# Layer 1's gate projection: eight strips of 512-column matmuls in pairs by Strassen's seven block products

## The chip, the cores and the metric

The kernel runs on one core of one Trainium2 chip. The metric is the device time of one execution in microseconds (us); lower is better. Before the change three runs took 1444.09, 1445.64 and 1447.06 us, median 1445.64.

Engines are named as in the profile: PE (TensorE, matrix multiply), PEld (its loading of the stationary operand), DVE (VectorE), ACT (ScalarE), POOL (GpSimd), and SP (SyncE), whose queue issues all the DMAs that matter here.

## The reference

A trunk of two layers over a sequence of 1024 tokens, width 1024, one batch. Each layer is a pre-norm with adaLN modulation from a conditioning vector c, a mixer with a SiLU gate, an output projection and a gated residual. Layer 0 is differential attention, layer 1 multi-head latent attention:

```python
def _modulation(c, ada_w, ada_b):
    mod = jax.nn.silu(c) @ ada_w + ada_b
    shift, scale, gate = jnp.split(mod[:, None, :], 3, axis=-1)
    return shift, scale, gate
...
def _mla(h, positions, w_in, q_a_norm_g, w_q_b, kv_a_norm_g, w_kv_b, w_out):
    proj = h @ w_in
    q_a, c_kv, k_pe, z = jnp.split(proj, [384, 640, 704], axis=-1)
    q = _rmsnorm(q_a, q_a_norm_g) @ w_q_b          # 8 heads of 128 + 64
    kv = _rmsnorm(c_kv, kv_a_norm_g) @ w_kv_b      # 8 heads of 128 (k) + 128 (v)
    ...                                            # rope on q_pe and k_pe, softmax attention
    o = o.reshape(b, s, MLA_WIDTH) * jax.nn.silu(z)
    return o @ w_out
...
    x = x + gate * y
```

The matmul that the change touches is z = h @ w_z: 1024 tokens by 1024 columns, contracted over 1024.

## The kernel before

**Precision.** Every projection is computed from split operands: a float is written as hi + lo, both in the fp32r format, and `mm3` issues three matmuls, hi·hi, hi·lo and lo·hi, into one PSUM bank (L178 to L180). So each operand needs a split: ACT casts it to hi, then POOL (for weights, L223 and L224) or DVE subtracts hi from it to get lo.

**Layout.** The normed input of layer 1 lies in SBUF transposed, as `h1[k][half]`: k = 0 to 7 are blocks of 128 channels, half = 0 or 1 the first or last 512 tokens, each a pair (hi, lo) of tiles of 128 x 512. A strip of weights makes 128 output columns: two raw tiles of 128 x 512 (`wraw`, two buffers, in `wst`) are loaded, split, and multiplied with the eight k of each half: 24 matmuls of 128 x 512 to one result in PSUM. Results lie with output columns on partitions and tokens along the free axis.

**Stages of layer 1**, in the order of PE's program, on which the stages lie one behind the other:

1. *The latent strips* (`lora`, L1215 on): strip 0 is k_pe (rope follows, `kp_half`), 1 to 3 are q_a, 4 and 5 are c_kv. ACT copies each result to `craw` and squares it (`csq`), DVE adds the squares up (`csum`). After the last strip of a latent and half, `norm` sums over partitions on PE (`cps`, eight small matmuls), takes the inverse root (DVE `c_w`, POOL `rq_y`), and spreads it over all partitions by a trip through DRAM: a store `bc_d` and a broadcast load `bc_s`. Then `rest` multiplies (`craw`, DVE), and splits into hi (ACT) and lo (POOL), which stay in SBUF as `CQ` and `CK` until attention 1. The four cps stand, on PE, among the strips that follow: `half_and_norm` runs what waits in `norms` at k = 4 of the next half strip. Two fall among the c_kv strips, the third and fourth at the start of the gate strips.
2. *The gate strips* (`z1_strip`, h = 0 to 7): per half 24 matmuls, a tanh on ACT, one DVE operation that reads the result from PSUM, and a store to `zS` in DRAM. Between the strips, `gen_gate` computes layer 1's residual gate: eight loads of 512 KB and eight DVE dot products of 128 x 1024 (L428).
3. *The first half of v* (`v1_tile`, eight tiles of six matmuls): each is split into `v_hl` (three buffers) by ACT and DVE and stored to `vS` in DRAM, 512 KB a store.
4. *The first strips of attention 1*: rope part of q (`w_qr`), k and q of head 0 (`w_kn`, `w_qn`), the rest of v, and then the scores, a stream of softmax tiles in which PE transposes and multiplies without a break.

**What sets the order.** PE's work is written out in the program's text. The other engines' instructions are put into one in-order queue per engine when the program is built, by a scheduler that follows the text and the readiness of data as it models it; an engine doesn't go past an instruction that waits. SP's queue is in order as well: a DMA that waits for its source or for a free buffer holds the ones behind it.

Here is one PSUM detail that matters: strips take their banks in turn from five (two `acc`, three `accx`), so the sixth result after a given one needs its bank.

Of the kernel before, what the change touches and what calls it, by code (L numbers as in the profile page):

```python
# [27 lines left out]
NH = 8  # L28
# [50 lines left out]
def f32v(ap):  # L79
    return ap.bitcast(F32)  # L80
# [3 lines left out]
def trunk(ctx: ExitStack, tc: tile.TileContext, A, out):  # L84
# [61 lines left out]
    def part(name):  # L146
        lo, n = VEC[name]
        return vec[:, lo : lo + n]
# [1014 lines left out]
    def strip1(i, wpool=None):  # L1163
        return load_strip([A["w_s1"][i, f] for f in range(2)], [4, 4], wpool)
# [23 lines left out]


    stC = ExitStack()  # L1190
    cqp = pool(stC, "cq", side="right")
    CQ = [[(cqp.tile([P, HF], F32R, name=f"cqh{k}_{f}"), cqp.tile([P, HF], F32R, name=f"cql{k}_{f}")) for f in range(2)] for k in range(3)]
    CK = [[(cqp.tile([P, HF], F32R, name=f"ckh{k}_{f}"), cqp.tile([P, HF], F32R, name=f"ckl{k}_{f}")) for f in range(2)] for k in range(2)]
# [4 lines left out]
    st4 = ExitStack()  # L1198

    def kp_half(half, acc):  # L1200
        rot, fin = rope(wp, acc, half, 1.0)

        def g():
            rot()
            r = fin()
            hi = lr.tile([P, HF], F32R, name="kp_h", tag="kp_h", bufs=1)
            V.tensor_copy(hi, r)
            V.tensor_copy(KP[half][0:64], r[0:64])
            V.tensor_sub(KP[half][64:128], r[64:128], f32v(hi[64:128]))

        return g

    norms = []

    def half_and_norm(w, half, consume):  # L1215

        for k, _ in enumerate(gen_half(w, h1, half, consume)):
            if k == NORM_AT:
                for f in norms[:]:
                    norms.remove(f)  # L1220
                    f()

    def lora(idx, dst, gvec, width, ws=None, first=None):
        n = len(idx)
        craw = [[None, None] for _ in range(n)]
        sums = [None, None]
        def put(i, half, acc):
            t = lr.tile([P, HF], F32, name="craw", tag="craw", bufs=6)
            S.copy(t, acc)
            craw[i][half] = t  # L1230
            if i == 0:
                sums[half] = lr.tile([P, HF], F32, name="csum", tag="csum", bufs=2)
                S.activation(sums[half], acc, AF.Square)
            else:
                s2 = lr.tile([P, HF], F32, name="csq", tag="csq", bufs=1)
                S.activation(s2, acc, AF.Square)
                V.tensor_add(sums[half], sums[half], s2)

        def norm(half):
            pt = bank("tr", "cps", [P, 4, P])  # L1240
            for j in range(4):
                PE.matmul(pt[:, 0, j : j + 1], sums[half][:, j * P : (j + 1) * P], ones[:, 0:1], start=True, stop=True)
            wv = sm.tile([P, 4], F32, name="c_w")
            V.tensor_scalar(wv, pt[:, 0, 0:4], 1.0 / width, EPS, op0=ALU.mult, op1=ALU.add)
            y = rsqrt(wv, 4)
            _, rb = bcast_rows(lr, y, "cbc", 1)

            def rest():
                for i in range(n):
                    t = craw[i][half]  # L1250
                    tc.keep_in_program_order(V.scalar_tensor_tensor(
                        out=t3(t), in0=t3(t), scalar=gvec[:, i : i + 1], in1=rb, op0=ALU.mult, op1=ALU.mult))
                    hi, lo = dst[i][half]
                    S.copy(hi, t)
                    G.tensor_sub(lo, t, f32v(hi))
# [12 lines left out]

    def first_halves(put):

        g0 = kp_half(0, strip_half(w4[0], h1, 0))
        for _ in gen_half(w4[1], h1, 0, put):
            side.tick()
        side.flush()
        st3x.close()
        g0()
        kp_half(1, strip_half(w4[0], h1, 1))()

    lora((1, 2, 3), CQ, qag, QL, w4[1], first_halves)
    lora((4, 5), CK, kvg, KVL)  # L1280

    def z1_strip(h, extra=None):
        w = strip1(6 + h)
        if extra:
            extra()
        for half in range(2):
            def put(acc, half=half):
                gz = silu_gate(wp, acc)
                SP.dma_start(zS[h, half], gz)
            half_and_norm(w, half, put)  # L1290

    z1_strip(0)
    stL.close()
    stv = ExitStack()
    pv1 = pool(stv, "pv1", side="right")
    p4 = pool(st4, "p4")

    c2, c_fin = load_c(p4, p4.tile([P, D], F32, name="cth", tag="ada", bufs=2))
    c_fin()
    gates = gen_gate(1, lambda src: mod_load(src, p4, 2), c2)  # L1300
    next(gates)
    wk = [[None, None] for _ in range(2)]

    def load_wk(fh, wpool):
        for k in range(2):
            raw = p4.tile([P, HF], F32, name="wvr", tag="wvr", bufs=2)
            SP.dma_start(raw, A["w_v1"][k, fh])
            h_ = wpool.tile([P, HF], F32R, name="wvh", tag="wv1", bufs=4)
            l_ = wpool.tile([P, HF], F32R, name="wvl", tag="wv1", bufs=4)
# [9 lines left out]
            mm3(acc, ch[:, c_], cl[:, c_], wk[k][fh][0], wk[k][fh][1], k == 0, k == 1)  # L1319
        store_v(1, sp, acc, tt, fh, *buf)  # L1320

    for h in range(1, NH):
        next(gates)
# [4 lines left out]
    sth.close()  # L1328

# [74 lines left out]
    def attn1(h, fills, extra=None, late=None):  # L1404

        def open_(half):
            ctx_["gz"] = wst.tile([P, HF], F32, name="gz1", tag="gz", bufs=3)
            SP.dma_start(ctx_["gz"], zS[h, half])

        def close(half, o_, zz):  # L1410
            if late and half == 1:
                ctx_["late"] = late(o_, zz, ctx_["gz"])
                return
            o = ap.tile([P, HF], F32, name="o1", tag="o", bufs=2)
            V.scalar_tensor_tensor(out=o, in0=o_, scalar=0.5, in1=ctx_["gz"], op0=ALU.mult, op1=ALU.mult)
            V.reciprocal(zz, zz)
            finish(o, zz, 1, h, half, None, ap, None)
# [40 lines left out]
    for tt in v1_left:  # L1458
        v1_tile(tt, 1, ap, "pt", 6)
    stv.close()  # L1460
    for h in range(NH - 1):
        attn1(h, lambda i: FILL1[i])
        while late_q:
            late_q.pop(0)()
        stream1.step(sum(steps1[: h + 2]) - stream1.count)
    stw.close()
    stC.close()
    stO = ExitStack()
# [158 lines left out]
```

## Time and profile before

| what | us |
|---|---|
| median of three runs | 1445.64 |
| the profiled execution | 1448.22 |
| its span | 1446.4 |
| PE busy | 1396.9 |
| DVE, ACT, POOL busy | 858.4, 710.5, 605.0 |
| latent strips to gate strips (first cps at, first gate matmul at) | 829.7, 858.03 |
| gate strips to v (first matmul of v at) | 949.23 |
| first matmul of the qr strip | 960.43 |
| first scores of attention 1 | 985.86 |

PE's granted clock over the run was 0.995 of full speed. Times in the text are microseconds from the start of the span. In a row of a timeline the columns are start, duration, engine, line, operation, output<-inputs, partitions x elements, and in square brackets how long the engine had been idle and what released it. The line numbers before the prediction are those of the kernel before; L1216 and above in the order of the changed kernel are its own.

### The profile page before, as it was taken

Reading aid. Unit: us, or ns where it says so; the run is one execution under the profiler, and the core shown is the slowest. Engines: PE = TensorE matmul, PEld = TensorE weight load, DVE = VectorE, ACT = ScalarE, POOL = GpSimd, SP = SyncE. Lnnn points to the kernel's source line nnn. Section 1 sums busy time; section 2 is a strip of 40 time slices with the busy share of each in tenths; the row PEclk is TensorE's granted clock in tenths of the full one; section 3 lists DMA queues with packets and bytes.
Section 4 is the critical chain, followed back from the end, with each engine's and each line's share of the span. In section 5 each row is a group of like instructions: output and inputs, shape, how many; then the busy total and the mean of one; then the engine's idle time right before and its main releaser. Section 6 shows DMA issues by size and latency. Waiting matters only on the chain.

```text
span 1446.4 us, 20456 instructions
## 1 busy us (share of the span) xinstructions
PE 1396.9 (97%) x7424; PEld 1167.0 (81%) x7424; DVE 858.4 (59%) x1272; ACT 710.5 (49%) x1258; POOL 605.0 (42%) x484
## 2 busy tenths in 40 slices
PE   5999999999999999998999999998999999999997
PEld 4778788888888887887787878787888888888886
DVE  6656777767777767677344445134555555555365
ACT  5522366656565665566343332234454554545342
POOL 4416164656564655453551264321141321412473
PEclk9999999999999999999999999999999999999999
DMA  9787823333333324137653127367242332345574
GB/s 327 234 248 234 256 66 97 87 103 81 101 97 88 98 81 110 63 95 262 229 171 124 38 69 239 110 189 204 77 104 77 110 99 76 105 136 175 172 238 149
DMA packets 128470, 203.19 MB, mean 140 GB/s; under 512 B 18289, under 2 KB 55281, under 8 KB 128369
## 3 DMA queue, kind: packets, MB, share of 16 engines
q1 hardware_dynamic: 128368, 201.89, 45.6%
q8 instruction: 58, 0.95, 0.3%
q14 instruction: 44, 0.35, 0.1%
HBM read 132.68 MB, written 45.56 MB: 123 GB/s over the span
## 4 chain that ended last, share of the span: by engine, by line
PE 77%; DMA 7%; DVE 6%; ACT 3%; POOL 3%; issue 2%; SPq 2%; ACTq 0%; DVEq 0%; POOLq 0%
PE s L1397 10%; PE acc L180 8%; PE acc L179 8%; PE acc L178 8%; PE tr L376 7%; PE s L767 7%; PE pv L179 4%; PE pv L178 4%; PE pv L180 4%; PE oacc L178 4%; PE oacc L179 4%; PE oacc L180 4%; DMA ada<-in_ada_g 2%; DMA wvr<-in_w_v 2%; DMA vS<-v_hl 1%
## 5 line engine op out<-in xcount | busy, mean ns | idle before, releaser
L378 ACT CAST pth<-tr 128x512 fp32r<-128x512 f32 x256 | 150.3, 587 | 283.6 <-PE tr L376 280.0
L393 DVE TENSOR_REDUCE nm<-s 128x1 f32<-128x1024 f32 x192 | 234.0, 1219 | 73.6 <-PE s L767 64.0
L379 DVE TENSOR_TENSOR ptl<-tr,pth 128x512 fp32r<-128x512 f32 x256 | 176.2, 688 | 150.2 <-ACT pth L378 149.9
L224 POOL TENSOR_TENSOR wl<-wraw,wh 128x512 fp32r<-128x512 f32 (+2 forms) x94 | 116.8, 1244 | 243.4 <-ACT wh L223 216.2
L395 ACT ACTIVATE e<-s,nm 128x1024 f32<-128x1024 f32 x128 | 143.7, 1122 | 28.1 <-DVE nm L393 27.6
L376 PE MATMUL tr<-ident,e 128*128 128x128 f32 x1024 | 154.6, 273 | 1.9 <-DVE ptl L379 1.7
L376 PEld LDWEIGHTS tr<-ident,e 128*128 128x128 f32 x1024 | 121.5, 140 | 42.8 <-DVE ptl L379 19.2
L178 PE MATMUL acc<-h0h,wh 128*128 128x512 f32 x360 | 150.0, 417 | 2.0 <-DVE v_hl L356 1.9
L178 PE MATMUL pv<-pth,vt 128*128 128x256 f32 x512 | 147.4, 288 | 0.0
L179 PE MATMUL pv<-ptl,vt 128*128 128x256 f32 x512 | 145.5, 284 | 0.0
L180 PE MATMUL pv<-pth,vt 128*128 128x256 f32 x512 | 144.6, 282 | 0.0
L180 PE MATMUL acc<-h0h,wl 128*128 128x512 f32 x360 | 142.2, 395 | 0.5 <-POOL wl L224 0.5
L179 PE MATMUL acc<-h0l,wh 128*128 128x512 f32 x360 | 141.4, 393 | 0.0
L1007 POOL TENSOR_TENSOR wol<-wor,woh 128x512 fp32r<-128x512 f32 x64 | 85.8, 1361 | 84.4 <-ACT woh L1006 79.4
L178 PEld LDWEIGHTS pv<-pth,vt 128*128 128x128 f32 x512 | 97.6, 191 | 3.0 <-ACT pth L378 0.4
L179 PEld LDWEIGHTS pv<-ptl,vt 128*128 128x128 f32 x512 | 97.7, 191 | 2.6
L180 PEld LDWEIGHTS pv<-pth,vt 128*128 128x128 f32 x512 | 97.7, 191 | 0.1
L325 POOL TENSOR_TENSOR rp_sw<-rp_sw,sinT 128x512 f32<-128x512 f32 x42 | 55.2, 1314 | 80.6 <-DMA rp_sw<-rp_raw 77.6
L767 PE MATMUL s<-ks,qa 128*128 128x512 f32 x256 | 82.2, 402 | 3.5 <-DVE e L775 3.1
L775 DVE SCALAR_TENSOR_TENSOR e<-s,z,e 128x1024 f32<-128x1024 f32 x64 | 82.1, 1283 | 2.1
L223 ACT CAST wh<-wraw 128x512 fp32r<-128x512 f32 (+2 forms) x94 | 55.2, 587 | 55.8 <-PE acc L179 38.5
L320 POOL TENSOR_TENSOR rp_r<-rp_raw,cosT 128x512 f32<-128x512 f32 x38 | 49.4, 1302 | 78.5 <-ACT rp_raw L315 50.8
(469 smaller groups left out, 3281.7 us busy)
## 6 DMA issues: line engine op xcount, KB each, us to landing
wraw<-in_w_s SPq DMA_DIRECT2D x76, 256.0 KB, 2.8
ada<-in_ada_ss SPq DMA_DIRECT2D x32, 512.0 KB, 6.1
vS<-v_hl SPq DMA_DIRECT2D x32, 512.0 KB, 4.9
vt<-vS SPq DMA_DIRECT2D x32, 512.0 KB, 4.0
wor<-in_w_out SPq DMA_DIRECT2D x64, 256.0 KB, 3.9
rp_sw<-rp_raw SPq DMA_DIRECT2D x168, 64.0 KB, 2.0
bc_s<-bc_d SPq DMA_DIRECT2D x34, 256.0 KB, 4.0
ada<-in_ada_g SPq DMA_DIRECT2D x16, 512.0 KB, 5.2
```

The source lines that it names most:

```text
L178: PE.matmul(psum, ah, bh, start=first, stop=False)
L179: PE.matmul(psum, ah, bl, start=False, stop=False)
L180: PE.matmul(psum, al, bh, start=False, stop=last)
L224: sub = (V if pair_of else G).tensor_sub(l_[:, :n], raw[:, :n], f32v(h_[:, :n]))
L376: PE.transpose(tr[:, j, :], p[:, kt * P : (kt + 1) * P], ident)
L378: mk["S"] = S.copy(pth[kh][:, :, dst], tr).ins
L379: mk["V"] = V.tensor_sub(ptl[kh][:, :, dst], tr, f32v(pth[kh][:, :, dst])).ins
L393: mk["V"] = V.reduce_max(nm, s_ps, axis=AX.X, negate=True).ins
L395: mk["S"] = S.activation(e, s_ps, AF.Exp, bias=nm, scale=1.0, accum_out=zs).ins
L767: PE.matmul(s_ps[:, kc * HF : (kc + 1) * HF], src[:, c, ql], KS[h][kc][:, c, :], start=fst, stop=not fst)
L1007: in_turn(G.tensor_sub(lo, raw, f32v(hi)))
L1397: PE.matmul(s_ps[:, kc * HF : (kc + 1) * HF], lhs, rhs(kc), start=i == 0, stop=i == 4)
```

## The change

**The products.** The gate strips go in pairs. The contraction is cut into two halves of four k (q = 0, 1), the tokens into the two halves, and the columns of a pair into its two strips. With A = h1 (four blocks: A00 = `h1q(0,0)`, A01, A10 = `h1q(1,0)`, A11) and W (a11, a12 for the first strip, a21, a22 for the second), the four results of a pair come from seven products of four k each, in Winograd's form, in place of eight: 84 matmuls a pair, not 96. Per pair DVE makes four sums of weights from raw tiles (`z_weights`), and all seven weight blocks are split by ACT and POOL. DVE makes seven sums of results from PSUM; the first product is copied to SBUF (`zu`) by ACT; the tanh and the gating operation read sums in SBUF.

**The input sums.** Products 3 to 6 need T2, T3, T1 and T4, sums of the blocks of A, 16 tiles (hi, lo). Each `combo` takes two DVE subtractions (of the hi and of the lo parts), a DVE addition, a cast on ACT and a subtraction on POOL. They are set amid the latent strips, one a k step (`side.tick`).

**Room.** The sums take the place of `CQ` and `CK`: the latents are now split as soon as they are normed, stored to DRAM (`cS`, 20 tiles of 256 KB), and loaded again in pair 3, once products have freed tiles. The small tiles of these steps share a ring of six ("rp"). The weights of v (`load_wk`) come by way of `wraw`.

**The gate's dot products** move from between the gate strips to attention 1's heads 0 to 3: sixteen of 128 x 512, each with a load of 256 KB, two per two softmax steps, issued behind DVE's running work (`gate_steps`).

```diff
-    CQ = [[(cqp.tile([P, HF], F32R, name=f"cqh{k}_{f}"), cqp.tile([P, HF], F32R, name=f"cql{k}_{f}")) for f in range(2)] for k in range(3)]
+    TC = {n: [(ut(f"t{n}h", n == 1 and k > 1), ut(f"t{n}l", n == 1 and k > 1)) for k in range(4)] for n in (2, 3, 1)}
+    cS = dr.tile([5, 2, 2, P, HF], F32, name="cS")
...
+    def combo(dst, x, y):
+        hi, lo = dst
+        t, u = rpt("cmb_t"), rpt("cmb_u")
+        V.tensor_sub(t, f32v(x[0]), f32v(y[0]))
+        V.tensor_sub(u, f32v(x[1]), f32v(y[1]))
+        V.tensor_add(t, t, u)
+        S.copy(hi, t)
+        G.tensor_sub(lo, t, f32v(hi))
+
+    def combos():
+        for k in range(4):
+            a_, b_ = h1[k][0], h1[k + 4][0]
+            c_, d_ = h1[k][1], h1[k + 4][1]
+            combo(TC[1][k], c_, a_)
+            combo(TC[2][k], d_, TC[1][k])
+            combo(TC[3][k], d_, c_)
...
+            combo(TC[4][k], h1[k + 4][0], TC[2][k])
...
-                    hi, lo = dst[i][half]
+                    hi = rpt("c_h", F32R)
                     S.copy(hi, t)
-                    G.tensor_sub(lo, t, f32v(hi))
+                    G.tensor_sub(t.bitcast(F32R), t, f32v(hi))
+                    SP.dma_start(cS[dst + i, half, 0], f32v(hi))
+                    SP.dma_start(cS[dst + i, half, 1], t)
...
+    def z_weights():
+        for _ in range(NH // 2):
+            a11, a12 = zraw[:2]
+            yield split_raw(a11, 4)
+            yield split_raw(a12, 4)
+            a21, a22 = zraw[2:4]
...
+            V.tensor_add(s1, a21, a22)
+            V.tensor_sub(a21, a11, a21)
+            V.tensor_sub(a11, s1, a11)
+            V.tensor_sub(a12, a12, a11)
+            for t in (a11, a21, s1, a22, a12):
+                yield split_raw(t, 4)
...
+    def z_pair(p, late=lambda i: None):
+        u = rpt("zu")
+        S.copy(u, product(h1q(0, 0)))
+        acc = product(h1q(1, 0))
+        c_ = rpt("z11")
+        V.tensor_add(c_, acc, u)
+        gate_out(2 * p, 0, c_, c_)
+        V.tensor_add(u, product(TC[2]), u)
+        late(0)
...
+        acc = product(TC[3])
+        u3 = rpt("zu3")
+        V.tensor_add(u3, acc, u)
+        late(1)
+        acc = product(TC[1])
...
+        V.tensor_add(u3, product(TC[4]), u3)
+        gate_out(2 * p + 1, 0, u3, u3)
+        V.tensor_add(u, product(h1q(1, 1)), u)
+        gate_out(2 * p, 1, u, u)
...
-    for h in range(1, NH):
-        next(gates)
-        z1_strip(h, lambda: [load_wk(fh, wpool) for fh, wpool in enumerate((p4, pv1))] if h == NH - 1 else None)
+    def late_z(i):
+        if i == 0:
+            load_ck(CK, 3, [(k, half) for half in range(2) for k in range(2)])
+        if i == 1:
+            load_ck(CQ, 0, [(0, 0), (1, 0), (2, 0), (0, 1)])
+        if i == 2:
+            load_wk(0)
+            load_ck(CQ, 0, [(1, 1), (2, 1)])
+    z_pair(1)
+    load_wk(1)
+    z_pair(2)
+    z_pair(3, late_z)
```

Three places show how the change moves instructions.

DVE's queue from the end of the k_pe rope on, before (`kps` is the rope's last result, `csum` the sum of squares of which the third and fourth let the first two cps go, `c_w` what DVE does behind a cps):

```order
L1208 CAST kps_7011<-rp_r 64x512
L1209 TENSOR_TENSOR kps_7011<-rp_r,kp_h 64x512
L1237 TENSOR_TENSOR csum<-csum,csq 128x512 x2
L1244 TENSOR_SCALAR c_w<-cps 128x4
L1237 TENSOR_TENSOR csum<-csum,csq 128x512
```

and in the changed kernel (L1228 to L1230 are a combo's three operations, L1352 and L1353 sums of weights, L1280 is csum):

```order
L1216 TENSOR_TENSOR kps_7011<-rp_r,kp_h 64x512
L1228 TENSOR_TENSOR cmb_t<-h1h,h_0h 128x512
L1229 TENSOR_TENSOR cmb_u<-h1l,h_0l 128x512
L1352 TENSOR_TENSOR zs_8573<-zraw 128x512
L1230 TENSOR_TENSOR cmb_t<-cmb_t,cmb_u 128x512
L1353 TENSOR_TENSOR zraw<-zraw 128x512
L1228 TENSOR_TENSOR cmb_t<-h1h,t1h 128x512
L1229 TENSOR_TENSOR cmb_u<-h1l,t1l 128x512
L1228 TENSOR_TENSOR cmb_t<-h1h 128x512
L1230 TENSOR_TENSOR cmb_t<-cmb_t,cmb_u 128x512
L1229 TENSOR_TENSOR cmb_u<-h1l 128x512
L1280 TENSOR_TENSOR csum<-csum,csq 128x512
```

Behind these stand, up to the third csum, twelve more operations of combos and one csum; the csum of the first norm now has 24 two-input operations between itself and the last kps.

ACT's queue at pair 0 in the changed kernel (`c_h` is the hi part of a normed latent, `zu` the copy of product 1, `t4h` the hi part of T4, `wh` that of a weight block); before, there was no zu, and c_h had no result behind it that PE's banks wait for:

```order
L1231 CAST t4h<-cmb_t 128x512
L223 CAST wh<-zraw 128x512
L1279 ACTIVATE csq<-acc 128x512
L223 CAST wh<-zraw 128x512
L1297 CAST c_h<-craw 128x512 x2
L1385 COPY zu<-zacc 128x512
L1362 ACTIVATE zth<-z_8638 128x512
```

The copy of product 1 stands behind two casts that need the third norm's broadcast.

SP's queue around v, before:

```order
L202 DMA wraw<-in_w_qr 128x384
L1289 DMA zS<-gz 128x512 x2
L202 DMA wraw<-in_w_kn 128x256
L202 DMA wraw<-in_w_qn 128x384
L1289 DMA zS<-gz 128x512 x2
L202 DMA wraw<-in_w_kn 128x256
L202 DMA wraw<-in_w_qn 128x384
L1408 DMA gz_9534<-zS 128x512
L1289 DMA zS<-gz 128x512
L358 DMA vS_0_71<-v_hl 256x4x128 x8
```

and in the changed kernel (`cS` is the parked latents, `c2h` the conditioning vector for the moved dots):

```order
L1440 DMA ckh<-cS 128x512
L1440 DMA ckl<-cS 128x512
L1364 DMA zS<-zu_9203 128x512
L1364 DMA zS<-zu 128x512
L358 DMA vS_0_71<-v_hl 256x4x128 x8
L202 DMA wraw<-in_w_qr 128x384
L202 DMA wraw<-in_w_kn 128x256
L1470 DMA c2h<-in_c 128x512 x2
```

The loads of the weights of attention 1's first strips (qr, kn, qn) stood ahead of the eight stores of v; now they stand behind all eight.

More of the change, by code (lines that the diff above doesn't have):

```diff
@@ L1190, in trunk, with ut @@
     stC = ExitStack()
-    cqp = pool(stC, "cq", side="right")
-    CQ = [[(cqp.tile([P, HF], F32R, name=f"cqh{k}_{f}"), cqp.tile([P, HF], F32R, name=f"cql{k}_{f}")) for f in range(2)] for k in range(3)]
-    CK = [[(cqp.tile([P, HF], F32R, name=f"ckh{k}_{f}"), cqp.tile([P, HF], F32R, name=f"ckl{k}_{f}")) for f in range(2)] for k in range(2)]
+    up = pool(stC, "u", side="right")
+    def ut(name, spare=False, dt=F32R):
+        return up.tile([P, HF], dt, name=name, tag="us" if spare else "u", bufs=4 if spare else 20)
+    TC = {n: [(ut(f"t{n}h", n == 1 and k > 1), ut(f"t{n}l", n == 1 and k > 1)) for k in range(4)] for n in (2, 3, 1)}
+    cS = dr.tile([5, 2, 2, P, HF], F32, name="cS")
     stw = ExitStack()
@@ L1275, in first_halves @@
         st3x.close()
+        p4 = pool(st4, "p4")
         g0()
         kp_half(1, strip_half(w4[0], h1, 1))()
[L1279 to L1290, printed above, removed]
@@ L1292, in trunk, with z_fetch @@
-    z1_strip(0)
+        cg = combos()
+        for _ in range(16):
+            side.add(None, None, None, lambda: next(cg))
+    p4 = None
+    lora((1, 2, 3), 0, qag, QL, w4[1], first_halves)
+    zraw = []
+    def z_fetch(p, parts):
+        for m, f in parts:
+            raw = p4.tile([P, HF], F32, name="zraw", tag="zraw", bufs=6)
+            SP.dma_start(raw, A["w_s1"][6 + 2 * p + m, f])
+            zraw.append(raw)
+    lora((4, 5), 3, kvg, KVL)
+    side.flush()
+    z_fetch(0, ((0, 0), (0, 1), (1, 0), (1, 1)))
@@ new lines, in gate_out, with product @@
+    def gate_out(h, half, c_, dst):
+        th = wst.tile([P, HF], F32, name="zth", tag="gz", bufs=3)
+        S.activation(th, c_, AF.Tanh, scale=0.5)
+        V.scalar_tensor_tensor(out=dst, in0=th, scalar=1.0, in1=c_, op0=ALU.add, op1=ALU.mult)
+        SP.dma_start(zS[h, half], dst)
+    zw = z_weights()
+    zq = [next(zw), next(zw)]
+    ticks = [0]
+    def product(rhs):
+        hi, lo = zq.pop(0)
+        zq.append(next(zw, None))
+        acc = bank("acc", "zacc")
+        for k in range(4):
+            mm3(acc, hi[k], lo[k], *rhs[k], k == 0, k == 3)
+            ticks[0] += 1
+            if ticks[0] % 8 == NORM_AT:
+                run_norms()
+        return acc
@@ L1320, in v1_tile, with load_ck @@
         store_v(1, sp, acc, tt, fh, *buf)
-    for h in range(1, NH):
-        next(gates)
-        z1_strip(h, lambda: [load_wk(fh, wpool) for fh, wpool in enumerate((p4, pv1))] if h == NH - 1 else None)
+    CK, CQ = [[None, None] for _ in range(2)], [[None, None] for _ in range(3)]
+    def load_ck(dst, n0, order):
+        for i, half in order:
+            dst[i][half] = ut("ckh"), ut("ckl")
+            for j, t in enumerate(dst[i][half]):
+                SP.dma_start(f32v(t), cS[n0 + i, half, j])
+    def late_z(i):
[10 more added lines that the diff above has]
+    z_pair(3, late_z)
+    st4.close()
+    p4 = pool(st4, "p4v")
     for tt in range(NT):
@@ L1328, in trunk, with gate_steps @@
     sth.close()
+    cg2 = [ut("c2h", True, F32) for _ in range(2)]
+    gw = [ut("gwh", True, F32) for _ in range(2)]
+    gcol1 = sm.tile([P, KT], F32, name="gcol", tag="gcol", bufs=1)
+    def gate_steps():
+        for i in range(2):
+            SP.dma_start(cg2[i], A["c"][:, i * HF : i * HF + HF].to_broadcast([P, HF]))
+        yield
+        yield
+        for i in range(2):
+            with behind("S"):
+                S.activation(gw[i], cg2[i], AF.Tanh, scale=0.5)
+        yield
+        for i in range(2):
+            with behind("V"):
+                V.scalar_tensor_tensor(out=cg2[i], in0=gw[i], scalar=1.0, in1=cg2[i], op0=ALU.add, op1=ALU.mult)
+        for j in range(KT):
+            yield
+            for i in range(2):
+                SP.dma_start(gw[i], A["ada_g1"][j, :, i * HF : i * HF + HF])
+            yield
+            yield
+            js = slice(j, j + 1)
+            for i in range(2):
+                with behind("V"):
+                    mod_dot(gw[i], part("ada_bg1")[:, js] if i == 0 else gcol1[:, js], gcol1[:, js], cg2[i])
+        SP.dma_start(gateS[1].rearrange("(p j) -> p j", p=P), gcol1)
+    gate1 = gate_steps()
     st5 = ExitStack()
@@ L1465, in trunk @@
         stream1.step(sum(steps1[: h + 2]) - stream1.count)
+    assert next(gate1, 0) == 0
     stw.close()
```

61 lines of the change are left out of this document (43 added, 18 removed).

## The prediction

> **What bounds the kernel now.** I read the page first, then the waits of TensorE (PE) by stretch, then the busy time of all engines there.
>
> ```profile
> span 1446.4 us, 20456 instructions
> PE 1396.9 (97%) x7424; PEld 1167.0 (81%) x7424; DVE 858.4 (59%) x1272; ACT 710.5 (49%) x1258; POOL 605.0 (42%) x484
> ...
> PE 77%; DMA 7%; DVE 6%; ACT 3%; POOL 3%; issue 2%; SPq 2%; ACTq 0%; DVEq 0%; POOLq 0%
> ```
>
> PE is busy for 97% of the span: a matmul that vanishes is worth its spacing, and a wait put between matmuls costs its length. PE's waits from 780 to 1010 us (layer 1's strips up to attention 1), and in the last row from 986 to 1345 us (us in total, times, longest):
>
> ```profile
> PE vps L178 <- DVE qn_l L1349: 4.4, 1, 4.4
> PE acc L180 <- POOL wl L224: 1.5, 1, 1.5
> PE trh L482 <- DVE xfull L471: 1.5, 2, 0.8
> PE cps L1242 <- DVE csum L1237: 1.1, 1, 1.1
> ...
> PE s L1397 <- ACT qn_h L1348: 0.5, 1, 0.5
> ```
>
> Here is little stall to recover and much to lose. The windows show the helpers (busy PE, PEld, DVE, ACT, POOL; clock; DMA share; GB/s):
>
> ```profile
> 820.00:864.00 44.00, 42.87 (x202) 35.18 (x202) 14.44 (x16) 14.83 (x27) 22.95 (x17) 1.00 0.23 67
> 858.04:949.23 91.19, 89.65 (x394) 72.78 (x393) 29.93 (x42) 22.18 (x38) 32.13 (x25) 1.00 0.48 155
> 985.00:1145.00 160.00, 159.53 (x937) 135.56 (x936) 85.80 (x112) 79.71 (x145) 34.51 (x28) 0.99 0.37 108
> ```
>
> VectorE (DVE) looks idle for two thirds of 820 to 864, GpSimd (POOL) for half. The change puts its added work there.
>
> **What goes: 48 matmuls.**
>
> ```profile
> 858.03 0.39 PE L178 MATMUL acc<-h_0h,wh 128*128 128x512 f32 x1
> ...
> 949.23 0.39 PE L178 MATMUL vps<-wvh,ckh 128*128 128x512 f32 x1
> ...
> 960.43 0.39 PE L178 MATMUL acc<-cqh,wh 128*128 128x512 f32 x1
> ...
> L1242 PE MATMUL cps<-ones,csum x32: 164/250/250, 829.7 to 862.2; 128*128 128x1 f32 x32
> ```
>
> The gate strips run from 858.03 to 949.23. Less 1.5 us of stall and 0.8 for the one group of eight small sums (cps, last row) that fell into it, 384 matmuls take 88.9 us, 0.231 each. Eight strips of 48 become four pairs of 84: 48 x 0.231 = **11.1 us** go. The stalls of 1.5 and 1.1 us belong to an order that is gone, so at best 13.7 us go, and the v1 tiles start at 935.5 in place of 949.23.
>
> **What comes: block sums, on two engines that shut each other out.** Sixteen combos, each of three DVE operations with both inputs in SBUF, one cast on ScalarE (ACT) and one POOL subtraction, are due before products 3 to 6 of pair 0. Prices:
>
> ```profile
> 816.11 0.69 DVE L329 TENSOR_TENSOR rp_r<-rp_r,rp_sw 128x512 f32<-128x512 f32 x1 [7.60 <-POOL rp_sw L325]
> 816.72 0.69 DVE L1237 TENSOR_TENSOR csum<-csum,csq 128x512 f32<-128x512 f32 x1
> ...
> 818.10 0.69 DVE L1209 TENSOR_TENSOR kps<-rp_r,kp_h 64x512 fp32r<-64x512 f32 x1
> ...
> L224 POOL TENSOR_TENSOR wl<-wraw,wh 128x512 fp32r<-128x512 f32 (+2 forms) x94 | 116.8, 1244 | 243.4 <-ACT wh L223 216.2
> ```
>
> DVE starts one such operation 0.6 us after another; POOL's takes 1.25. Side by side they would fit. The two engines' timelines say that they don't run side by side:
>
> ```profile
> 853.30 1.55 DVE L1237 TENSOR_TENSOR csum<-csum,csq 128x512 f32<-128x512 f32 x1 [2.65 <-ACT csq L1236]
> ...
> 853.02 1.28 POOL L1255 TENSOR_TENSOR cql<-craw,cqh 128x512 fp32r<-128x512 f32 x1
> 854.26 1.71 POOL L224 TENSOR_TENSOR wl<-wraw,wh 128x512 fp32r<-128x512 f32 x1
> ...
> 709.17 3.31 DVE L1055 TENSOR_TENSOR xfull<-xfull,oy 128x512 f32<-128x512 f32 x2
> ...
> 708.92 5.97 POOL L1007 TENSOR_TENSOR wol<-wor,woh 128x512 fp32r<-128x512 f32 x4 [4.79 <-DMA wor<-in_w_out]
> ...
> L1237 DVE TENSOR_TENSOR csum<-csum,csq x6: 686/897/1553, 816.7 to 859.7; 128x512 f32<-128x512 f32 x6
> ```
>
> POOL's cql ends at 854.30; the csum that began at 853.30 ends 0.55 later, at 854.85; the wl after it ends at 855.97, 1.12 after the csum. Each waited for the other. At 709, four POOL operations (5.0 us) and two of DVE's (1.2) share 5.97 us, nearly their sum. So I add the two engines' times, as on one resource.
>
> [...] The trace agrees at 853 and 709; the mean csum (0.94 against 0.69) could also be read as a toll of 0.25 us an operation, by which 48 combo operations would cost 12 us in place of full turns, and the sum below would be near that of the first rival. [...]
>
> The walk, by the new order. The first combo starts behind the last kps, at 818.7. Up to the third csum, for which the first cps waits, stand 25 such DVE operations and 9 of POOL: 25 x 0.6 + 9 x 1.25 = 26.3, so 845. The cps stands 23 matmuls later than before (829.7 + 23 x 0.233 = 835), so PE stalls 10 us. Up to the last T4: 48 combo operations, 4 weight sums and 5 csum at 0.6, six craw at 1.1, against 33 POOL operations at 1.25 and three small ones at 1.0: 40.8 + 44.3 = 85 us, so **903**. PE would want T4, for product 6, at 872. The last norm's chain ends no sooner:
>
> ```profile
> 856.06 0.16 DVE L1244 TENSOR_SCALAR c_w<-cps 128x4 f32<-128x4 f32 x1 [1.21 <-PE cps L1242]
> ...
> 863.85 2.20 DVE L1251 SCALAR_TENSOR_TENSOR craw<-craw,vec,bc_s 128x512 f32<-128x512 f32 x2 [1.17 <-POOL rq_y L165]
> ...
> 866.08 0.62 ACT L1254 CAST ckh<-craw 128x512 fp32r<-128x512 f32 x1
> ```
>
> From cps to the second latent's cast went 855.8 to 866.7, 11 us, by way of DRAM. That cast (now c_h) stands ahead of pair 0's copy zu on ACT, and product 6 takes the bank that zu frees. Its cps waits for a csum behind nearly all combos, near 895.5, so zu is free near 907; product 6 and 7 take 24 x 0.233 = 5.6: pair 1 starts at 912.6, not 877.2 (the strips start at 858.0 less the 1.1 us stall and one cps group, and pair 0 holds 84 x 0.233 and two such groups): **35.4 us lost**. Pairs 1 to 3 need, in 19.4 us of PE each, 7 POOL and 4 DVE operations that exclude each other (11 us): nothing. So v1 starts at 912.6 + 58.3 = 970.9: **+21.7**. Bounds of pair 0's loss: 5.4 us, if only the norm's 11.3 us chain stands against the 5.9 us of PE work between cps and product 6, and some 45, if every small stretch of idle engines adds.
>
> **The stores of v1 ahead of the next weights.**
>
> ```profile
> 929.14 0.33 SPq L202 DMA_DIRECT2D wraw<-in_w_qr  x1
> ...
> 952.23 14.08 SPq L358 DMA_DIRECT2D vS<-v_hl x8
> ...
> 957.00 0.59 ACT L355 CAST v_hl<-vps 128x512 fp32r<-128x512 f32 x1 [2.79 <-DMA vS<-v_hl]
> ...
> wraw<-in_w_s SPq DMA_DIRECT2D x76, 256.0 KB, 2.8
> ```
>
> Now the qr weights are asked for 20 us before v1; in the new order they stand behind the eight vS stores, of which each third waits for a buffer. The eighth is issued 17.1 us after v1's start (949.23 to 966.3); 2.8 to land and 0.5 to cast make 20.4; a subtraction and transfers in the way make it 22. PE ends v1's tiles after 11.2 (960.43). Idle: **11 us**, between 9 and 13.
>
> An idle PE returns at a lower clock:
>
> ```profile
> 977.90 0.39 PE L180 MATMUL vps<-wvh,ckl 128*128 128x512 f32 x1
> 982.71 0.79 PE L178 MATMUL vps<-wvh,ckh 128*128 128x512 f32 x1 [4.42 <-DVE qn_l L1349]
> ...
> 989.58 0.39 PE L179 MATMUL vps<-wvl,ckh 128*128 128x512 f32 x1
> ```
>
> From 982.71 to 989.58, 17 matmuls take 6.9 us where 17 x 0.233 = 4.0 would do: 2.9 us after one idle of 4.4. This old stall, 4.4 + 2.9, ended a chain of the q rope whose loads queued with the eight vS stores; behind them, and with the slow clock ahead, I take the rope to be in time. In its place 11 + 2.9: net **+6.6** (+13.9 if the old stall stays). Another **2.9** follows pair 0's long stall. [...]
>
> **Gate dots, parking, reload.**
>
> ```profile
> L428 DVE CUSTOM_DVE_ANT_0 ada<-ada,c,vec x8: 1274/1285/2164, 882.5 to 903.4; 128x1024 f32<-128x1024 f32 x8
> ```
>
> Eight dots of 1.285 leave the gate strips, where nobody waited for them; sixteen halves, two tanh and two products go amid attention 1: 18 x 0.65 = 12 us of DVE in 160, where it is busy for 86. Each can hold up a softmax step by 0.65; PE waited 0.5 us in all there. I take **1**, between 0 and 5. The latents cost SyncE's queue 20 stores and 20 loads of 256 KB; the loads start when pair 3's products free tiles, c_kv first, and must land in the some 10 us until v1: 8 x 256 KB are 7 us at 300 GB/s (a slice of the page has 327). I take nothing, and up to 3 us for the range.
>
> **Sum.** 21.7 + 2.9 + 6.6 + 1 = +32.2 on the profiled run of 1448.2 (span 1446.4 and 1.8 around it), which was 2.6 above the median of 1445.6: 1477.8. **Forecast 1478.**
>
> **Rivals.**
> First, the toll only: the engines give way in small pieces, and pair 0 waits by chains alone. Walking the same order with each engine's own times, where a combo's next use waits for its cast (0.6) and subtraction (1.25), gives 2 and 1 us at the first two cps, 3.5, 2.6 and 5.9 at products 4, 5 and 6, some 16 in sum: v1 at 951, the rest as above, +12.5, **1458**. For it: most csum rows are lengthened by 0.2 only. Against: 709.
>
> Second, faster, and one mechanism: the block sums keep ahead. If T4 is complete before 872, pair 0 costs nothing, since neither cps nor zu waits. The place is DVE between 818 and 872; the point from which it decides is 5 us of loss there, since 13.7 - 6.6 - 1 = 6 are left to give. Then -13.7 + 6.6 + 1 = -6, **1439**. For it: 14 of 44 us DVE busy. Against: 85 us of turns in 53.
>
> Third, the qr weights are also in time: the stores leave faster than v1's old 14 us. Then with pair 0 hidden -13.7 and the 7.3 us of the rope's stall kept: **1432**. With pair 0 as forecast it is 1471, inside my range.
>
> Fourth, pair 0 loses only the norm's 5.4: -6 + 5.4, **1445**: no change.
>
> **How the numbers follow.** Forecast 0.56 (its own range 1466 to 1490), toll 0.22, pair 0 hidden 0.08, that and the weights 0.05, norm alone 0.09. A measurement of this kernel tells 0.2%, 2.9 us, from no change: 1442.7 to 1448.5. Faster: 0.08 + 0.05 = 0.13. Same: the norm's case, 0.07 of its 0.09. Slower: 0.80. The range, 1446 to 1489, leaves out the faster cases and a little at the top.
>
> **What would show it.** Right: PE waits of cps on csum of about 10 us near 840; idle at products 3 to 6 on POOL's t lo, ACT's zu or T2 to T4, 20 us or more; DVE combos of 1.2 to 1.9 us beside POOL; one wait of 9 to 13 us for wraw of qr behind vS; clock near 0.5 behind both; matmuls 0.231 apart in pairs 1 to 3; attention 1 as long as before within 3 us. Wrong: combos at 0.6 to 0.7 us beside POOL's, pair 0 below 30 us, qr's strip directly behind v1, or waits in pairs 1 to 3.

## The result: slower, 1479.3 us against 1445.7

The changed kernel took 1479.32 us (four runs, 1478.25 to 1482.17), the kernel before 1445.68: a ratio of 1.0236, 95% interval 1.0218 to 1.0255. The forecast was 1478, with a range of 1446 to 1489.

The page of the profiled execution, the same lines as before:

```profile
span 1478.3 us, 20674 instructions
PE 1399.4 (95%) x7376; PEld 1167.2 (79%) x7376; DVE 949.5 (64%) x1381; ACT 729.4 (49%) x1291; POOL 655.6 (44%) x512
...
PE 80%; DVE 7%; DMA 6%; ACT 2%; issue 2%; POOL 1%; SPq 1%; ACTq 0%; DVEq 0%; POOLq 0%
```

There are 48 matmuls fewer, and yet PE is busy for 2.5 us more: a busy microsecond is no longer a microsecond at full clock (granted clock over the run 0.978, before 0.995). In the view of PE's waits from 780 to 1040 us (us in total, times, longest) only the wait for xfull is as before; cps waited for csum before too, but 1.1 us:

```profile
PE zacc L178 <- ACT csq L1279: 12.1, 2, 11.3
PE acc L178 <- ACT wh L223: 12.0, 1, 12.0
PE cps L1285 <- DVE csum L1280: 9.8, 2, 9.0
PE zacc L178 <- ACT zu L1385: 2.0, 1, 2.0
PE trh L482 <- DVE xfull L471: 1.5, 2, 0.8
PE zacc L178 <- ACT wh L223: 1.3, 1, 1.3
PE zacc L180 <- POOL wl L224: 1.0, 1, 1.0
```

The zacc of lines 1, 4, 6 and 7 and the cps are the pair 0 stage, 26 us; line 2 is the qr strip, 12 us. PE's timeline gives the places, with the idle time in square brackets:

```profile
843.45 1.84 PE L1285 MATMUL cps<-ones,csum 128*128 128x1 f32 x8 [9.03 <-DVE csum L1280]
...
891.13 0.80 PE L178 MATMUL zacc<-t3h,wh 128*128 128x512 f32 x1 [11.30 <-ACT csq L1279]
893.10 1.83 PE L1285 MATMUL cps<-ones,csum 128*128 128x1 f32 x8 [0.75 <-DVE csum L1280]
...
909.29 0.50 PE L178 MATMUL zacc<-t4h,wh 128*128 128x512 f32 x1 [1.96 <-ACT zu L1385]
...
916.47 0.39 PE L178 MATMUL zacc<-h_0h,wh 128*128 128x512 f32 x1
...
974.43 0.39 PE L178 MATMUL vps<-wvh,ckh 128*128 128x512 f32 x1
...
997.46 0.79 PE L178 MATMUL acc<-ckh,wh 128*128 128x512 f32 x1 [11.99 <-ACT wh L223]
...
1019.40 0.62 PE L1561 MATMUL s<-kn_h,qn_h 128*128 128x512 f32 x2
```

The first cps, product 4, the third cps within it, product 6, pair 1, v, the qr strip, the first scores. V starts 25.2 us later than before, the scores 33.5 later, and the span is 31.9 longer: the loss is made between 818 and 1020, and attention 1 gives 1.6 back: before, the clock behind the old stall was still 0.50 from 986 to 988, while the first scores ran, which now run at full clock. Its windows, before and after (160 us each, before from the first scores, after from 7 us ahead of them; busy PE, PEld, DVE, ACT, POOL, then the clock), show that the moved dots cost PE nothing:

```profile
985.86:1145.86 160.00, 159.53 (x942) 135.76 (x941) 86.24 (x113) 80.38 (x147) 34.51 (x28) 0.99 0.37 107
```

```profile
1012.00:1172.00 160.00, 159.93 (x938) 136.08 (x937) 98.83 (x145) 81.52 (x148) 38.97 (x30) 1.00 0.48 139
```

DVE carries 12.6 us more there, 13.2 if the second window starts at the first scores as well (forecast: 12), and PE waits no longer.

Where the first wait comes from is seen where DVE's and POOL's timelines of the changed kernel are laid side by side:

```profile
818.09 1.78 DVE L1229 TENSOR_TENSOR cmb_u<-h1l,h_0l 128x512 f32<-128x512 f32 x1
819.79 0.68 DVE L1352 TENSOR_TENSOR zs<-zraw 128x512 f32<-128x512 f32 x1
820.39 0.68 DVE L1230 TENSOR_TENSOR cmb_t<-cmb_t,cmb_u 128x512 f32<-128x512 f32 x1
820.99 1.77 DVE L1353 TENSOR_TENSOR zraw<-zraw 128x512 f32<-128x512 f32 x1
...
896.37 0.69 DVE L1230 TENSOR_TENSOR cmb_t<-cmb_t,cmb_u 128x512 f32<-128x512 f32 x1
```

```profile
817.89 1.42 POOL L224 TENSOR_TENSOR wl<-wraw,wh 128x512 fp32r<-128x512 f32 x1 [2.65 <-ACT wh L223]
820.66 1.56 POOL L224 TENSOR_TENSOR wl<-wraw,wh 128x512 fp32r<-128x512 f32 x1 [1.34 <-ACT wh L223]
822.18 1.73 POOL L1232 TENSOR_TENSOR t1l<-cmb_t,t1h 128x512 fp32r<-128x512 f32 x1
...
897.89 1.65 POOL L1232 TENSOR_TENSOR t4l<-cmb_t,t4h 128x512 fp32r<-128x512 f32 x1
```

The same kind of DVE operation takes 0.68 us where it gets its turn at once and 1.67 to 1.79 where it first waits out a POOL operation: the one at 818.09 waits for the wl that ends at 819.31. Of the TENSOR_TENSOR rows with two SBUF inputs in this stretch none lies between. The whole stretch in one window:

```profile
817.50:897.10 79.60, 56.26 (x224) 44.43 (x223) 72.93 (x67) 25.78 (x47) 55.05 (x35) 0.83 0.24 77
```

67 DVE and 35 POOL operations: with the prices of an undisturbed one, 67 x 0.6 = 40 us and 35 x 1.25 = 44 us. Side by side they would need 44; one after the other they need 84, and the stretch is 79.6 (a few of them, c_w and rq_y, are smaller than these prices). Their busy times add up to 128, since each counts its waiting for the other.

### The profile page after: what moved, and what is told of

Its sections match the earlier page's. It is cut to its first block, busy times and chain, and to the rows that moved or that the text cites. A ratio compares the mean times of both kernels' runs of the same rounds, so it can differ in the third digit from the quotient of the medians.

```text
span 1478.3 us, 20674 instructions
## 1 busy us (share of the span) xinstructions
PE 1399.4 (95%) x7376; PEld 1167.2 (79%) x7376; DVE 949.5 (64%) x1381; ACT 729.4 (49%) x1291; POOL 655.6 (44%) x512
## 4 chain that ended last, share of the span: by engine, by line
PE 80%; DVE 7%; DMA 6%; ACT 2%; issue 2%; POOL 1%; SPq 1%; ACTq 0%; DVEq 0%; POOLq 0%
PE s L1561 10%; PE acc L180 7%; PE acc L178 7%; PE acc L179 7%; PE tr L376 7%; PE s L767 7%; PE pv L179 4%; PE pv L178 4%; PE pv L180 4%; PE oacc L178 4%; PE oacc L180 4%; PE oacc L179 4%; PE zacc L178 2%; PE zacc L179 2%; PE zacc L180 2%
## 5 line engine op out<-in xcount | busy, mean ns | idle before, releaser
L224 POOL TENSOR_TENSOR wl<-wraw,wh 128x512 fp32r<-128x512 f32 (+2 forms) x78 | 98.7, 1267 | 211.1 <-ACT wh L223 180.6
L767 PE MATMUL s<-ks,qa 128*128 128x512 f32 x256 | 82.1, 402 | 3.3 <-DVE e L775 2.9
L775 DVE SCALAR_TENSOR_TENSOR e<-s,z,e 128x1024 f32<-128x1024 f32 x64 | 82.1, 1283 | 2.1
L767 PE MATMUL s<-ks,qb 128*128 128x512 f32 x256 | 80.9, 394 | 0.0
```

What stands on the lines that cost most here:

```text
L224: sub = (V if pair_of else G).tensor_sub(l_[:, :n], raw[:, :n], f32v(h_[:, :n]))
L767: PE.matmul(s_ps[:, kc * HF : (kc + 1) * HF], src[:, c, ql], KS[h][kc][:, c, :], start=fst, stop=not fst)
```

## The experiments

The kernels ran on different chips, on which the kernel before took medians of 1446 to 1450 us. So kernels are compared by their ratio to the kernel before on the same chip (the expectations give times for the first chip: ratio x 1445.7), and inside a profile by two stretches: from the start of the last kps (the end of the k_pe rope, where the block sums begin) to v's first matmul, and from there to the first scores.

| kernel | ratio (95%) | kps to v, us | v to scores, us |
|---|---|---|---|
| before | 1 | 131.1 | 36.6 |
| changed | 1.0236 (1.0218 to 1.0255) | 157.7 | 45.0 |
| combos' lo on DVE | 1.0193 (1.0154 to 1.0233) | 152.8 | 44.0 |
| early qr weights | 1.0187 (1.0143 to 1.0231) | 157.9 | 37.4 |
| combos' POOL work left out | 1.0144 (1.0094 to 1.0194) | 144.8 | 44.2 |
| combos' lo and early qr | 1.0152 (1.0110 to 1.0195) | 154.2 | 36.4 |
| all lo on DVE | 1.0136 (1.0093 to 1.0180) | 145.9 | 44.6 |
| plain first pair | 1.0182 (1.0138 to 1.0225) | 151.9 | 43.4 |
| plain, lo, qr | 1.0117 (1.0059 to 1.0175) | 152.0 | 32.6 |
| plain, qr | 1.0128 (1.0062 to 1.0193) | 152.7 | 32.9 |
| late norm | 1.0202 (1.0169 to 1.0234) | 154.3 | 45.0 |
| fewer turns | 1.0020 (1.0004 to 1.0036) | 132.8 | 36.5 |
| fewer turns, plain | 0.9948 (0.9932 to 0.9965) | 125.0 | 32.1 |
| the same, loads behind v's | 0.9927 (0.9913 to 0.9941) | 124.9 | 31.8 |

**The combos' lo on another engine.**

```diff
         S.copy(hi, t)
-        G.tensor_sub(lo, t, f32v(hi))
+        V.tensor_sub(lo, t, f32v(hi))
```

> The sixteen subtractions that make the lo parts of T1 to T4 run on DVE instead of POOL. Theory of turns (a DVE operation with two SBUF inputs and a POOL operation exclude each other, so their times add up): sixteen turns of 1.25 us become sixteen of 0.6, the sum of turns up to the last T4 falls by about 10 us, and the time with it: 1467 to 1471 us against 1479; DVE operations of 1.7 to 1.8 us become rarer. Rival, a small toll and long chains: DVE gets 10 us more work, the chains get shorter by 0.65 us a combo: 1477 to 1483. Rival, ACT's order alone (product 4 waits for csq behind the casts of T4, product 6 for zu behind c_h): unchanged, 1478 to 1480.

In the second kernel that line is `S.copy(lo, t)`:

> The sixteen subtractions on POOL are left out; a cast on ACT fills the lo tiles in their place, with values that are not the lo parts. Theory of turns: sixteen turns of 1.25 us go and none comes: 20 us less up to the last T4, of which the last norm's round trip may keep some: 1459 to 1465 us, and below the run with the subtractions on DVE by 5 to 10 us. Rival, toll and chains: a combo's chain gets 0.65 us shorter, ACT has 10 us more: 1474 to 1482, and above or equal to the run with the subtractions on DVE only by what DVE's 10 us cost there. Rival, ACT's order alone: ACT has more ahead of csq and zu: 1479 or more.

DVE got sixteen operations more and the time still fell, by 4.9 us from kps to v; with POOL's part gone and nothing put on DVE, by 12.9. In ratio, 0.4% and 0.9%. That orders the two as the theory of turns has it, and against "ACT's order alone". The sizes are half to two thirds of what I expected, and both times lie above their range (by ratio 1473.6 and 1466.5): of 10 us fewer turns some came back as DVE standing idle (2.3 us at 852 for a weight's lo on POOL, 1.4 at 861 and 3.65 at 897 for casts). With the subtractions on DVE, PE's first wait for csum fell from 9.0 to 2.8 us, but product 4's for csq rose from 11.3 to 17.2. The interval of the first overlaps with the changed kernel's, so alone it would prove little.

**The weights of the qr strip ahead of the stores of v.**

```diff
+    q0raw, k0raw = fetch_strip([A["w_qr"][0]], [3]), fetch_strip([A["w_kn"][0]], [2])
+    wq0 = split_strip(q0raw)
     for tt in range(NT):
         v1_tile(tt, 0, p4)
...
-    stream1 = Stream(gen_strips(items))
+    items[1] = (lambda: k0raw, *items[1][1:])
+    stream1 = Stream(gen_strips(items, wq0))
```

> The weights of the qr and the first kn strip are asked for ahead of the eight vS stores, and qr's is split ahead of v's last tiles. Theory: the wait of 12.0 us and the slow clock behind it (2.9 us) go; the 4.4 us wait of the rope that the kernel before had may come back with its 2.9: 1464 to 1473 us. Rival: the loads are held by their buffer or by the reload of the latents, and the wait only gets another name: 1476 to 1480.

> The subtractions of the combos on DVE and the early qr weights together. If the two losses are separate, the gains add up: 1452 to 1464 us. If one hid the other, the time is that of the better one alone, 1464 to 1471.

SP's queue in the changed kernel, then PE's longest remaining wait in that stage in this one:

```profile
977.78 14.53 SPq L358 DMA_DIRECT2D vS<-v_hl  x8
992.40 0.66 SPq L202 DMA_DIRECT2D wraw<-in_w_qr  x1
```

```profile
PE acc L178 <- ACT wh L223: 3.1, 1, 3.1
```

From v to the scores it takes 37.4 us in place of 45.0, near the 36.6 of before: the 12.0 us wait is gone, and a 3.1 us one, for the next strip's weights, has come. The run with both edits has both gains: 1.0152 is 0.84% below 1.0236, against 0.43% and 0.49% apart, and in the two stretches 3.5 and 8.6 us, 12.1 together, against 4.9 and 7.6 apart. So the two losses are separate, though the time (by ratio 1467.7) lies in the range given for a hidden one: each gain was smaller than that range assumed, and the ratios alone, known to 0.4%, would not decide it.

**No subtraction on POOL in the stretch.** `split_raw` subtracts on DVE from the c_kv strips to pair 0, and so do the latents and the combos:

```diff
-        sub = (V if pair_of else G).tensor_sub(l_[:, :n], raw[:, :n], f32v(h_[:, :n]))
+        sub = (V if pair_of or on_v[0] else G).tensor_sub(l_[:, :n], raw[:, :n], f32v(h_[:, :n]))
```

> All subtractions of the stretch run on DVE: those of the combos, of the latents and of the weights of the c_kv strips and of pair 0, so that POOL has nothing there but two small inverse roots. Theory of turns: DVE operations of 1.7 to 1.8 us vanish between 818 and 900, and against the run with the combos' subtractions alone on DVE, 17 turns of 1.25 us become 0.6: 11 us fewer turns, half of them given back in waits for casts as in that run: 1466 to 1471 us. Rival, DVE's load itself is the bound (no turns): DVE has 10 us more work: 1480 to 1487. Rival, ACT's order: as that run, 1475 to 1478.

From kps to v 145.9, 11.8 us less than the changed kernel, though DVE does all of POOL's work as well. Of 96 DVE rows in the first 65 us from the last kps on one takes over 1.3 us; in the changed kernel it is 18 of 52, and two groups of three `craw`. This expectation could have gone furthest wrong (up to 1487). But it also shows what the turns do not explain: with POOL out, the last lo of T4 was complete 71.2 us after the first block sum, in place of 82.1, and 102 DVE operations fill that time (idle 6.5 us). What is left of the lateness is mostly DVE's own work.

**A plain first pair.** The first two strips by four half strips of 24 matmuls (the expectation says eight), as before the change:

```diff
+    z1_strip(0)
+    z_fetch(1, ((0, 0), (0, 1), (1, 0), (1, 1)))
+    z1_strip(1)
...
-    z_pair(0)
```

> The first two gate strips are computed plainly (eight half strips of 24 matmuls in all, 96 in place of 84), the other three pairs by seven products. Theory of turns: nothing of the block sums changes, but PE asks for T2 some 22 us later; the loss of some 39 us shrinks by about that, and 2.8 us of matmuls come back: 1458 to 1464 us. The round trip of the third norm no longer stands ahead of a bank that a product waits for. Rival, a loss that goes along (a chain through the gate outputs or the weight sums): 1476 to 1482.

> Plain first pair, the combos' subtractions on DVE, and qr's weights early. If the three losses are separate: the plain pair takes about 19 us off, the early weights 7, the subtractions 4 to 10 of what is then left of pair 1's waits: 1443 to 1453 us, near the kernel before. If pair 1 still waits for the sums: 1455 to 1462.

> Plain first pair and qr's weights early, the combos' subtractions still on POOL. By turns it stands 4 to 10 us above the run that has them on DVE: 1450 to 1458. If the subtractions' engine no longer matters once PE asks later, both are the same within 1.5 us.

All three missed: 22 more us until T2 is wanted brought 5.8 us. The waits of the first of them say why (the second row is mostly the qr strip, 12.5 us):

```profile
PE cps L1285 <- DVE csum L1280: 20.8, 3, 11.2
PE acc L178 <- ACT wh L223: 13.2, 2, 12.5
```

PE no longer waits for any T, but for csum: the sums of squares of c_kv stand on DVE behind nearly all combos, and the cps that need them stand in PE's program, wherever the products are. In the kernel that also has the combos' lo on DVE, PE waits 9.1 us for csq and 8.1 for gz, 5.8 of them because DVE reaches gz only behind a `craw` that waits for its broadcast. The kernels "plain, lo, qr" and "plain, qr", which differ in the engine of the combos' subtractions, are 1.5 us apart, too little for their intervals. So with turns as they are, being wanted later is worth little: PE stands behind a norm, not behind a product.

**The norms of c_kv later.**

```diff
-                    norms.append(lambda half=half: norm(half))
+                    (held if dst else norms).append(lambda half=half: norm(half))
...
     z_pair(0)
+    norms += held
+    z_pair(1)
```

> One edit on the changed kernel: the two norms of c_kv (the third and fourth cps, their trip through DRAM, the casts c_h) are called in pair 1, not around pair 0; their values are first read in pair 3. Theory: of pair 0's loss of 39 us the last 9 to 10 were the norm's round trip (T4 is complete at 899.5, product 6 starts at 909.3), the rest turns: 1468 to 1472 us against 1479.3, and product 6 then waits for T4's lo on POOL. Rival, the place of the csum in DVE's queue is nearly all of the loss, since product 4 and 5 need no T4: 1450 to 1460. Rival, the norm doesn't matter: 1478 to 1481.

By ratio (1474.9) a miss for all three: 3.4 us from kps to v, and an interval that overlaps with the changed kernel's. The wait for zu is gone, and counted from the last kps product 6 started 10.1 us earlier; but pair 1 lost most of that again, with 3.3 us of waits for weights at 935 and, behind them, matmuls 0.43 us apart in place of 0.23 until 941.4. And product 4 still waits 11.4 us for csq, whose bank ACT can't free since it stands behind casts of T4 that wait for DVE (ACT idle for 5.5 us until the one at 890.58, csq at 891.11). Neither the norm nor the products alone decide; what stands on DVE, or behind it on another engine, is late with it.

**Fewer turns.** T2 = d - T1, T3 = T2 - a and T4 = b - T2 from the unsplit sums, two DVE operations each in place of three, with all subtractions on DVE, c_kv's norms in pair 1 and qr's weights early:

```diff
-            combo(TC[2][k], d_, TC[1][k])
+            V.tensor_sub(t2, d_[0], t1)
+            V.tensor_add(t2, t2, d_[1])
+            split_t(TC[2][k], t2)
-            combo(TC[3][k], d_, c_)
+            V.tensor_sub(t3, t2, a_[0])
+            V.tensor_sub(t3, t3, a_[1])
+            split_t(TC[3][k], t3)
```

> All the found causes at once: all subtractions of the stretch on DVE, nine DVE sums for each k in place of twelve (T2, T3, T4 are made from the unsplit sums), c_kv's norms in pair 1, qr's weights early. By turns, some 80 operations of 0.6 us stand on DVE between the k_pe rope and the last T4, none on POOL: T4 at 868 to 875, where PE wants it at 872: pair 0 loses 2 to 10 us: 1434 to 1444 us, faster than the kernel before. Rival, casts and banks hold what turns no longer hold: 1446 to 1460.

> The same with the first pair computed plainly: 12 matmuls (2.8 us) more, 22 us more until T2 is wanted. If the run without the plain pair still waits for sums by more than 2.8 us, this one is the faster: 1435 to 1441. If not, it is 2 to 3 us slower than that run.

The window from the first block sum to the last of this kernel, and two of its rows:

```profile
821.20:881.10 59.90, 50.90 (x216) 40.23 (x215) 55.00 (x86) 27.40 (x49) 4.19 (x3) 0.92 0.31 102
```

```profile
824.70 0.68 DVE L1361 TENSOR_TENSOR zraw<-zraw 128x512 f32<-128x512 f32 x1
...
880.35 0.69 DVE L1228 TENSOR_TENSOR t4l<-cmb,t4h 128x512 fp32r<-128x512 f32 x1
```

86 DVE operations now stand where there were 67, and take 60 us in place of 80: POOL has three. From kps to v it is 132.8, 24.9 us less than the changed kernel. By ratio (1448.6) it is 5 us above the top of the expected range and within that of the rival, casts and banks, and slower than the kernel before by 0.2%; four edits came at once here, so no single one has this gain to itself. Product 3 waits 8.3 us for T2, since the last k of T1 to T4 stand on DVE behind six `craw`. There the plain first pair does its work: 125.0 us, 7.8 less, and a ratio of 0.9948 (1438.2, in the expected range).

**Loads behind v's.** In that kernel attention 1 waited 3.15 us for its first tile of v (the two kernels with a plain first pair and early qr weights had 2.4 and 2.1); in SP's queue two loads for the moved dots (c2h) stood ahead of it. The view of SP's queue of that kernel:

```profile
988.65 2.77 SPq L1491 DMA_DIRECT2D c2h<-in_c  x2
991.52 0.71 SPq L202 DMA_DIRECT2D wraw<-in_w_kn  x1
992.28 0.95 SPq L369 DMA_DIRECT2D vt<-vS  x2
```

The last kernel starts `gate_steps` four steps later and keeps the weights' subtractions on DVE through pair 3.

> The fastest run so far (plain first pair, fewer sums, all subtractions on DVE, late norm, early qr weights) with two edits: the gate strips' weight subtractions stay on DVE through pair 3, so that POOL has none in the strips, and the two loads of the conditioning vector for the moved dots (2.8 us of SP's queue at 988.65) are asked for behind the first loads of v. Theory: its waits of 1.9 us (product 3 of a pair for a weight's lo on POOL) and of 3.1 us (attention 1's first product with v for its load) go: ratio to the kernel before 0.990 to 0.993, against 0.9948. Rival, the load of v is late by itself, since its stores are: 0.994 to 0.996, the wait stays. Rival, DVE is full with the weights' subtractions: above 0.996.

```profile
PE zacc L180 <- DVE wl L226: 1.4, 1, 1.4
PE pv L178 <- DMA vt<-vS: 0.9, 1, 0.9
PE zacc L178 <- ACT wh L225: 0.8, 1, 0.8
```

The wait for v fell from 3.15 to 0.9 us, that for a weight's lo from 1.9 to 1.4. 1439.5 us against 1450.2 on the same chip, 0.9927 (0.9913 to 0.9941), is the fastest kernel here, faster than before. Against 0.9948 the intervals overlap, so the step itself isn't settled by the times.

## Why the prediction was right, and where its sizes were off

**The matmuls.** Pairs 1 to 3 run from 916.47 to 974.43: 58.0 us, forecast 58.3. The product itself does what it should; the 11.1 us of 48 matmuls were gained and could not be seen in the span.

**The turns.** The first cps ran at 843.5 with 9.0 us of wait (forecast 845, 10); T4 was complete at 899.5 (903); product 6 started at 909.3 (907), for zu as forecast. The rival of a small toll on each operation (its terms add up to 15, not the 16 given, so some 1457) is refuted: the rows of the stretch take 0.68 or 0.69 us, or 1.67 to 1.79, and nothing between. That the turns cost time is shown by the run that took POOL's subtractions out of the stretch: 11.8 us less from kps to v, though DVE did them as well. They are not the whole loss: what remained there goes mostly with DVE's own added work, and it went in the kernel with fewer sums and later norms (86 operations in 60 us).

**The split between waits and clock was off.** I had pair 0 and the first cps lose 35.4 us in waits and 2.9 by the clock. The waits are 26.2; v still started 25.2 us late, where 24.6 was forecast, since the clock took the rest. The place was off too: product 6, where I had most of it, waited 2.0 us. Windows of 4 us of the changed kernel, PE busy throughout (the last three numbers are the clock, the DMA share and GB/s):

```profile
894.00:898.00 4.00, 4.00 (x13) 3.32 (x13) 3.96 (x6) 0.62 (x1) 3.30 (x4) 0.50 0.00 0
902.00:906.00 4.00, 4.00 (x15) 3.42 (x15) 1.44 (x3) 0.00 (x0) 1.01 (x1) 0.50 0.40 131
918.00:922.00 4.00, 4.00 (x19) 3.21 (x18) 4.00 (x6) 2.19 (x4) 3.30 (x3) 1.00 0.68 219
```

Of the 13 and 15 matmuls in the first two, 8 and 7 are of 512 columns, the others the small ones of cps; 19 fit at full clock. By matmuls counted against 0.23 us each, 820 to 926 lost about 13 us this way. Where the next product waits for an engine anyway, a slow PE and a waiting PE are the same time under two names, so the sum of both came out right.

**A wait I hadn't named.** Product 4's 11.3 us went to csq. I had looked for the end of the lateness at T4 and zu; the same turns reached PE earlier by way of a bank that ACT had not read. My description of the order also had PE's work as the text writes it: the third cps, called in the last c_kv strip, stands in the built program in product 4.

**The qr strip.** 12.0 us of wait (forecast 11), from v to scores 8.3 us longer (6.6). The weights landed 4.4 us after their issue, not 2.8; the queue had just given out eight stores of 512 KB, which may be why, but no run tests it. The old stall of the rope did go.

**Attention 1.** Forecast +1, measured none (the 1.6 us less are the clock's); the parking in DRAM cost PE no wait in any row.

**The rivals** "pair 0 loses only the norm" and "the block sums keep ahead" are refuted for this kernel: T4 was complete at 899.5, not before 872, and PE waited 26.2 us in that stage.

## What to carry to other kernels

Before putting element-wise work on two idle engines, look in the trace for rows in which both run at once: here a DVE operation on two SBUF inputs and a POOL operation took turns (1.67 to 1.79 us in place of 0.68 where DVE had to wait), so the free time of the two was one resource, not two: 40 and 44 us of work took 79.6. Moving POOL's subtractions of the stretch to DVE was a gain, 11.8 us from kps to v, although DVE was the busier. And a gain in matmuls is only as good as its helpers' queues: one late engine in order (DVE) delayed norms, banks and casts that had nothing to do with the new products (PE waited 9.0 us for csum, 11.3 for csq).

## What the runs showed of the hardware that I had not expected

The clock came back late where short interruptions followed a long wait. After the 11.3 us of idle it was at 0.50 from 891 until 907.1, through waits of 0.75 and 0.83 us and two groups of small matmuls; and the wait of 1.96 us that ended at 909.29 cost another stretch at half clock, not at once but from 910.5 to 913.9 (PE alone; busy, then clock, DMA share and GB/s):

```profile
845.64:849.05 3.41, 3.41 (x9) 0.50 0.02 1
849.05:850.00 0.95, 0.95 (x5) 1.00 0.22 15
...
903.66:907.08 3.42, 3.42 (x9) 0.50 0.09 21
907.08:910.49 3.41, 1.45 (x6) 1.00 0.52 132
910.49:913.90 3.41, 3.41 (x10) 0.50 0.74 273
913.90:916.00 2.10, 2.10 (x10) 1.00 0.52 196
```

After 9.0 us of idle without such interruptions it was back at 849.05, 5.6 us after PE's start at 843.45. From 849.05 to 907.08 are 58.03 us, 17 times 3.413: in this run the clock changed on a grid of 3.41 us, and each of these two restarts ended with the first step that PE filled with large matmuls alone. The 5.6 us are what was left of one step, 2.19 us, and a full one of 3.41; the restart with interruptions, in which no earlier step was free of a wait or of small matmuls, took 16 us (891.13 to 907.08).

A POOL operation also pays: 1.27 us alone, mostly 1.4 to 1.8 beside DVE operations with two SBUF inputs. DVE operations that read PSUM were spared: `z<-zacc,zu` took 0.68 us at 910.78, while POOL ran from 909.02 to 912.00, and all 23 sums from zacc that overlapped with a POOL operation up to 980 took 0.68 or 0.69. Of the two readings that the prediction weighed, full turns and a toll of 0.25 us on each operation, the trace shows full turns for the TENSOR_TENSOR operations with two SBUF inputs from 817.5 to 897.1: 0.68 or 0.69 us, or 1.67 to 1.79.
